# Hybrid recurrence and convolution layer: weight splits and part of the row preparation moved from VectorE and ScalarE to GpSimd in the first sweep

## The chip, the cores and the metric

The kernel runs on one core of one Trainium2 chip. The metric is the device time of one execution in microseconds. The core has TensorE (PE in the rows; its weight loads are PEld), VectorE (DVE), ScalarE (ACT), GpSimd (POOL) and SyncE (SP), which here only issues DMAs. Each engine works through a queue of its own in order; semaphores order the engines among each other.

## The reference, cut to what matters

One layer on 4096 tokens of width 1024, with 256 context tokens ahead of them:

```
h = rmsnorm(x, norm_g) * (1 + scale(c)) + shift(c)
q, zf, zb, v, ga, u, ug, gb = split(h @ w_in)            # 8 groups of 512 columns
o = hgrn2_bidir(q, v, zf, zb)                            # 4 heads x 128, both directions
y = conv_tail(depthwise_conv(u * sigmoid(ug), width 31)) # rows and columns of the 64-wide grid
m = concat(head_rmsnorm(o) * silu(ga), y * silu(gb)) @ w_out
out = rmsnorm(x + gate(c) * m, final_norm_g)
```

The recurrence is S_t = diag(f_t) S_(t-1) + k_t v_t^T, o_t = S_t^T q_t, forward and backward over the tokens, all in float32.

## The kernel before

The tokens pass in two sweeps. The **first sweep** goes forward over NB = 16 blocks of TB = 256 tokens. For each block it makes the projections q, v, the two forget gates, u and ug, runs the forward recurrence of the block, and the row part of the convolution. The **second sweep** goes back over 32 groups of 128 tokens: the backward recurrence, the gates ga and gb, the column part of the convolution, the output projection and the last norm. Projections have float32 accuracy by splitting both operands into a high and a low float16 part and running three passes of matmuls (`proj_cm` L284, `proj_v` L295).

The work of one block b in the first sweep is a set of generators, stepped in turn by `merge` in the proportion of given weights: `hgrn(b)`, `row_conv(b)`, the projections of block b+1, `prep_rows` for block b+2 (it starts after half its share of steps), and a side job from the table `side`, which prepares weights for the second sweep. What `merge` writes is the program order; the framework's scheduler then orders each engine's queue by its own timing model.

`prep_rows` (L248 to L271) loads two tiles of 128 rows. Each tile goes: SP loads `xt` (L253), ACT squares it (L256, which writes a scrap into `hl`), DVE and POOL form the reciprocal root (L257, L78; L81, L84, L85 on POOL, 128x1 each), then for two halves of 512 columns DVE multiplies (L263) and adds (L265), ACT casts to float16 (L266), DVE subtracts for the low part (L268), and SP transposes both parts into `aT` by DMA (L271).

The side jobs are: block 1 `gate_rows`, block 2 `scale_w2` twice, blocks 3 to 6 of the table `split_w2` for two weight groups, blocks 7 to 10 `split_wo` twice. Between `merge` and the scheduler the queues run about one block ahead of the table; by the trace the `split_w2` writes lie in stretches b2 to b5 and the `split_wo` writes in b6 to b9. `split_w2` loads 256 rows of a weight group into `wst`, scales and splits them (ACT L183, DVE L184) and writes both parts to DRAM as `w2d`. `split_wo` loads a gate row and a piece of `w_out` into `gw`, multiplies them (DVE L907 or L909), casts (ACT L910), subtracts (DVE L911) and writes `wod`. The tiles `hl` of all three jobs share one buffer (tag A, a single buffer), and `xt`, `wst` and `gw` share two. So the next user of `hl` waits until the DMA that read the one before is done.

The recurrence `hgrn(b)` has levels: ACT copies keys into `km` (L751), PE makes scores (L726), DVE scales and doubles (L758, L759), then two steps across larger halves (PE L779, ACT L789 and L798, DVE L768 and L769). At its end `split_keys` splits the keys into float16 parts (ACT L555, DVE L556, tile K) and SP transposes them by DMA back into X (L557); PE needs the transposed keys for `pu` (L573). SP also issues the tile writes `qbd` (X, L806), in queue order with the weight writes and loads. A stretch "b4" below is the time from one block's first write of `opd` (L825) to the next.

```
proj.append(project_v(aTs[b], d))
if b + 1 < NB:
    proj.append(project_fq(aTs[b + 1], blk[b + 1]))
if b + 2 < NB:
    proj.append(project_gu(b + 1, aTs[b + 1], blk[b + 1]))
gens.append((2 * N_UV if late_gu else N_V + N_FQ + N_GU, chain(*proj)))
if b in side:
    gens.append((26, chain(*side[b])))
if b + 2 < NB:
    gens.append((2 * N_ROWS, chain(idle(N_ROWS), prep_rows((b + 2) * TB, aTs[b + 2]))))
merge(*gens)
```

Of the kernel before, what the change touches and what calls it, by code (L numbers as in the profile page):

```python
# [9 lines left out]
F32 = mybir.dt.float32  # L10
# [4 lines left out]
ALU = mybir.AluOpType  # L15
# [24 lines left out]
R_NG, R_BM, R_LB, R_HG, R_CB, R_LG, R_LBI = 0, 8, 32, 48, 52, 56, 60  # L40
# [33 lines left out]
def rsqrt(nc, pool, out, v, n, tag, eng=None):  # L74

    eng = eng or nc.gpsimd
    y, t, h = out, pool.tile([P, n], F32, tag=tag + "t", name=tag + "t"), v
    nc.vector.tensor_scalar(y.bitcast(I32), v.bitcast(I32), -0.5, float(0x5F3759DF), ALU.mult, ALU.add)  # L78
    if n == 1:
        h = pool.tile([P, n], F32, tag=tag + "h", name=tag + "h")  # L80
        eng.tensor_scalar(h, v, -0.5, 0.0, ALU.mult, ALU.add)  # L81
    for _ in range(3):
        if n == 1:
            eng.tensor_scalar(t, y, y, h, ALU.mult, ALU.mult)  # L84
            eng.tensor_scalar(y, t, 1.5, y, ALU.add, ALU.mult)  # L85
        else:
            eng.tensor_tensor(t, y, y, ALU.mult)
            eng.tensor_tensor(t, t, v, ALU.mult)  # L88
            eng.tensor_scalar(t, t, -0.5, 1.5, ALU.mult, ALU.add)
            eng.tensor_tensor(y, y, t, ALU.mult)  # L90
# [8 lines left out]
def hymba_block(  # L99
# [3 lines left out]
    nc = tc.nc  # L103
# [12 lines left out]
    def const(shape, dt=F32, name=None):  # L116
        return cp.tile(shape, dt, tag=name, name=name)
# [6 lines left out]
    vec = const([P, NROW], name="vec")  # L124
# [34 lines left out]
    rwall = const([P, 8, 2], name="rwall")  # L159
# [17 lines left out]
    def split_chunk(hi, lo, st, g, dve=False):  # L177

        rw = rwall[:, g, 0:1]
        if dve:  # L180
            nc.vector.tensor_scalar(hi, st, rw, None, ALU.mult)
        else:
            nc.scalar.activation(hi, st, AF.Copy, scale=rw)  # L183
        nc.vector.scalar_tensor_tensor(lo, st, rw, hi, ALU.mult, ALU.subtract)  # L184

    def win_rows(g, k, n):
        return w_in[k * P : (k + n) * P, 512 * g : 512 * g + 512].rearrange("(k p) n -> p k n", p=P)
# [4 lines left out]
    with ExitStack() as s1:  # L192
# [55 lines left out]
        def prep_rows(r0, aT):  # L248

            for i in range(2):  # L250
                t = e1.tile([P, D], F32, tag="xt", name="xt", bufs=2)
                hl = e1.tile([P, 2, D], F16, tag="A", name="hl")
                nc.sync.dma_start(t, x[r0 + i * P : r0 + (i + 1) * P, :])  # L253
                yield
                ssq = sm.tile([P, 1], F32, tag="xssq", name="xssq")
                nc.scalar.activation(hl[:, 0, :].bitcast(BF16), t, AF.Square, accum_out=ssq)  # L256
                nc.vector.tensor_scalar(ssq, ssq, 1.0 / D, EPS, ALU.mult, ALU.add)  # L257
                r = sm.tile([P, 1], F32, tag="xr", name="xr")
                rsqrt(nc, sm, r, ssq, 1, "xq")
                yield  # L260
                for sl in (slice(0, 512), slice(512, D)):
                    ts = t[:, sl]
                    nc.vector.scalar_tensor_tensor(ts, ts, r, gs[:, 0, sl], ALU.mult, ALU.mult)  # L263
                    yield
                    nc.vector.tensor_tensor(ts, ts, gs[:, 1, sl], ALU.add)  # L265
                    nc.scalar.copy(hl[:, 0, sl], ts)  # L266
                    yield
                    nc.vector.tensor_tensor(hl[:, 1, sl], ts, hl[:, 0, sl], ALU.subtract)  # L268
                    yield
                for j in range(2):  # L270
                    nc.sync.dma_start_transpose(aT[:, j, :, i * P : (i + 1) * P], hl[:, j, :])  # L271
# [206 lines left out]
        gs = m1.tile([P, 2, D], F32, name="gs")  # L478
# [407 lines left out]
        def split_w2(g, i):  # L886

            t = e1.tile([P, 2 * 512], F32, tag="xt", name="wst", bufs=2)
            hl = e1.tile([P, 2, 2 * 512], F16, tag="A", name="hl")
            nc.sync.dma_start(t.rearrange("p (k n) -> p k n", n=512), win_rows(g, 2 * i, 2))  # L890
            yield
            split_chunk(hl[:, 0, :], hl[:, 1, :], t, g)
            nc.sync.dma_start(w2d[g][i], hl)
            yield

        def split_wo(k):

            for n in range(2):
                sl = slice(512 * n, 512 * n + 512)
                gw = e1.tile([P, 2, 512], F32, tag="xt", name="gw", bufs=2)  # L900
                hl = e1.tile([P, 2, 512], F32R, tag="A", name="hl")
                nc.sync.dma_start(gw[:, 0, :], gtd[:, sl])
                nc.sync.dma_start(gw[:, 1, :], w_out[k * P : (k + 1) * P, sl])
                yield
                w = gw[:, 1, :]
                if k < 4:
                    nc.vector.scalar_tensor_tensor(w, w, vec[:, R_HG + k : R_HG + k + 1], gw[:, 0, :], ALU.mult, ALU.mult)  # L907
                else:
                    nc.vector.tensor_tensor(w, w, gw[:, 0, :], ALU.mult)  # L909
                nc.scalar.copy(hl[:, 0, :], w)  # L910
                nc.vector.tensor_tensor(hl[:, 1, :], w, hl[:, 0, :].bitcast(F32), ALU.subtract)  # L911
                for i in range(2):
                    nc.sync.dma_start(wod[i][n][:, k, :], hl[:, i, :].bitcast(F32))
                yield

        side = {1: [gate_rows()], 2: [scale_w2(G_GA), scale_w2(G_GB)]}
        for i in range(4):
            side[3 + i] = [split_w2(G_GA, i), split_w2(G_GB, i)]
            side[7 + i] = [split_wo(2 * i), split_wo(2 * i + 1)]
# [35 lines left out]
        aTs[1] = new_aT(1)  # L955
        fq0 = chain(project_fq(aTs[0], blk[0]), project_gu(0, aTs[0], blk[0]))
        merge((N_CST, context_states(*cur["c"])), (N_FQ + N_GU, fq0), (5 * (N_LW - 8) // 3, lw), (N_ROWS, prep_rows(TB, aTs[1])))
        for b in range(NB):
            d = blk[b]
            if b < NB - 2:  # L960
                nc.sync.dma_start(aTd[b], aTs[b])
            late_gu = b == NB - 1
            if late_gu:
                late["gu"] = wp.tile([P, 2, T], F32, tag="pair", name="gu_all")
            gens = [(N_HGRN, hgrn(b, d)), (N_CONV * 5 // 4, chain(idle(N_CONV // 4 if late_gu else 0), row_conv(b, d)))]
            proj = [project_gu(b, aTs[b], d)] if late_gu else []
# [9 lines that stand above are left out]
                aTs[b + 2] = new_aT(b)  # L976
                gens.append((2 * N_ROWS, chain(idle(N_ROWS), prep_rows((b + 2) * TB, aTs[b + 2]))))
            if b == NB - 1:
                gens.append((N_W2, load_w2()))
            merge(*gens)  # L980
# [248 lines left out]
```

## Time and profile before

| what | value |
|---|---|
| median of 3 runs | 2219.68 us (2218.23 to 2222.2) |
| profiled execution | 2215.77 us |
| its span on the core | 2214.0 us |
| PE busy | 2083.6 us (94%) |
| DVE busy | 1749.6 us (79%) |
| ACT busy | 996.3 us (45%) |
| POOL busy | 458.5 us (21%), 1146 instructions |

The span is the time between the first and the last record of the core; the profiled execution's own time is 1.8 us above it and 3.9 us below the median of the runs. Busy time of an engine is the sum of its instructions without waits; the share is of the span. The page's slices of the span give the granted clock of TensorE in tenths, and it reads 9 nearly throughout.

### The profile page before, as it was taken

Reading aid. Unit: us, or ns where it says so; the run is one execution under the profiler, and the core shown is the slowest. Engines: PE = TensorE matmul, PEld = TensorE weight load, DVE = VectorE, ACT = ScalarE, POOL = GpSimd, SP = SyncE. Lnnn points to the kernel's source line nnn. Section 1 sums busy time; section 2 is a strip of 40 time slices with the busy share of each in tenths; the row PEclk is TensorE's granted clock in tenths of the full one; section 3 lists DMA queues with packets and bytes.
Section 4 is the critical chain, followed back from the end, with each engine's and each line's share of the span. In section 5 each row is a group of like instructions: output and inputs, shape, how many; then the busy total and the mean of one; then the engine's idle time right before and its main releaser. Section 6 shows DMA issues by size and latency. Waiting matters only on the chain. (4 is left out here: it accounts for less than half of the span.)

```text
span 2214.0 us, 54678 instructions
## 1 busy us (share of the span) xinstructions
PE 2083.6 (94%) x22334; PEld 1642.5 (74%) x22334; DVE 1749.6 (79%) x4270; ACT 996.3 (45%) x2310; POOL 458.5 (21%) x1146
## 2 busy tenths in 40 slices
PE   6999999999998999999999999978999999999997
PEld 3777778778777778778788876766677766667776
DVE  5988887897797887887898778888787887777754
ACT  4944545545535445445544543433333333333343
POOL 1110101110110110101110100044433344433332
PEclk8999999999999999999999999989999999999999
DMA  9436165324325335343322317332323322332322
GB/s 363 133 84 163 55 169 149 104 79 134 102 68 177 109 99 172 98 115 97 85 61 68 64 59 234 107 130 94 110 91 108 102 96 91 100 98 99 114 96 72
DMA packets 221476, 251.65 MB, mean 114 GB/s; under 512 B 143812, under 2 KB 147736, under 8 KB 216744
## 3 DMA queue, kind: packets, MB, share of 16 engines
q1 hardware_dynamic: 220104, 239.67, 36.4%
q0 software_dynamic: 1120, 8.49, 1.0%
q8 instruction: 175, 2.87, 0.5%
q14 instruction: 77, 0.63, 0.1%
HBM read 137.99 MB, written 76.55 MB: 97 GB/s over the span
## 5 line engine op out<-in xcount | busy, mean ns | idle before, releaser
L284 PEld LDWEIGHTS <-w 128*128 128x128 f16 x4704 | 455.8, 98 | 60.5 <-issue 2.6
L706 DVE SCALAR_TENSOR_TENSOR yr<-gu,convw,yr 128x224 f32<-128x224 f32 (+2 forms) x900 | 356.6, 444 | 0.0
L1048 DVE SCALAR_TENSOR_TENSOR ycs<-gu_all,convw,ycs 128x256 f32<-128x256 f32 (+2 forms) x828 | 343.9, 469 | 0.0
L284 PEld LDWEIGHTS <-pair 128*128 128x128 f16 x3168 | 308.5, 99 | 39.4 <-issue 0.6
L1146 PE MATMUL py<-wo,yh 128*128 128x512 f32 x1024 | 282.1, 413 | 3.8 <-ACT yh L1130 3.8
L81 POOL TENSOR_SCALAR xqh<-xssq 128x1 f32<-128x1 f32 x30 | 12.5, 418 | 1017.7 <-DVE xssq L257 1017.7
L1146 PEld LDWEIGHTS py<-wo,yh 128*128 128x128 f32 x1024 | 189.0, 192 | 43.8 <-ACT yh L1130 4.4
L284 PE MATMUL ps_z<-aT,pair 128*128 128x256 f16 x1632 | 191.1, 277 | 0.0
L1015 PE MATMUL ps_gb<-aT,w 128*128 128x256 f16 x1536 | 190.1, 273 | 0.0
L284 PE MATMUL ps_z<-aT,w 128*128 128x256 f16 x1632 | 188.3, 274 | 1.9 <-DVE aT L242 1.4
L295 PE MATMUL pv<-w,aT 128*128 128x512 f16 x816 | 184.4, 379 | 1.4 <-DVE gu L670 1.4
L751 ACT COPY km<-X 128x512 f32<-128x512 f32 x160 | 107.9, 675 | 168.2 <-DVE X L759 167.9
L284 PE MATMUL ps_u<-aT,w 128*128 128x256 f16 x1536 | 180.6, 274 | 0.0
L1003 PE MATMUL ps_ga<-w,aT 128*128 128x512 f16 x768 | 178.6, 385 | 0.0
L284 PE MATMUL ps_g<-aT,w 128*128 128x256 f16 x1536 | 178.3, 273 | 0.0
L284 PE MATMUL ps_q<-aT,pair 128*128 128x256 f16 x1536 | 172.9, 273 | 0.0
L1015 PEld LDWEIGHTS <-w 128*128 128x128 f16 x1536 | 145.5, 98 | 31.5 <-issue 15.8
L295 PEld LDWEIGHTS <-aT 128*128 128x128 f16 x816 | 77.4, 98 | 88.3 <-issue 1.6
L1146 PE MATMUL py<-wo,yl 128*128 128x512 f32 x512 | 139.6, 402 | 0.0
L1003 PEld LDWEIGHTS <-aT 128*128 128x128 f16 x768 | 72.8, 99 | 88.1 <-issue 10.4
L314 ACT ACTIVATE f<-f,lbv,oml 128x128 f32<-128x128 f32 x272 | 113.0, 485 | 0.1
L1146 PEld LDWEIGHTS py<-wo,yl 128*128 128x128 f32 x512 | 95.0, 192 | 19.1
(268 smaller groups left out, 3360.7 us busy)
## 6 DMA issues: line engine op xcount, KB each, us to landing
xt<-in_x_dram SPq DMA_DIRECT2D x64, 512.0 KB, 3.5
out_dram<-xt SPq DMA_DIRECT2D x31, 512.0 KB, 2.7
aTd<-aT SPq DMA_DIRECT2D x14, 1024.0 KB, 4.7
aT<-aTd SPq DMA_DIRECT2D x14, 1024.0 KB, 5.8
wst<-in_w_in_dram SPq DMA_DIRECT2D x16, 512.0 KB, 4.5
wod<-hl SPq DMA_DIRECT2D x32, 256.0 KB, 3.0
qbd<-X SPq DMA_DIRECT2D x31, 256.0 KB, 2.1
ubd<-ub SPq DMA_DIRECT2D x31, 256.0 KB, 2.0
```

Of the source, the lines that this page charges most:

```text
L81: eng.tensor_scalar(h, v, -0.5, 0.0, ALU.mult, ALU.add)
L284: nc.tensor.matmul(ps[:, j, :], w[:, wi, k, (ct + j) * P : (ct + j + 1) * P], aT[:, ai, k, :], start=n == 0, stop=n == 23)
L295: nc.tensor.matmul(pv, aT[:, ai, k, i * P : (i + 1) * P], W[G_V][:, wi, k, :], start=n == 0, stop=n == 23)
L314: nc.scalar.activation(fa, fa, AF.Identity, scale=oml[:, d, ct + j : ct + j + 1], bias=lbv[:, d, ct + j : ct + j + 1])
L706: nc.vector.scalar_tensor_tensor(ar[i][:, :, lo:hi], gr[i][:, :, lo + dl : hi + dl], convw[:, i, j : j + 1], ar[i][:, :, lo:hi], ALU.mult, ...
L751: nc.scalar.copy(fap(km, 0, kd), fap(Xs[gi], 0, ks))
L1003: nc.tensor.matmul(ps, aT[:, ai, k, i * P : (i + 1) * P], Wa[:, wi, k, :], start=n == 0, stop=n == 23)
L1015: nc.tensor.matmul(ps[:, j, :], Wb[:, wi, k, (ct + j) * P : (ct + j + 1) * P], aT[:, ai, k, :], start=n == 0, stop=n == 23)
L1048: nc.vector.scalar_tensor_tensor(ya, gu_all[:, i, (lo + dl) * GW : (hi + dl) * GW], convw[:, 2 + i, j : j + 1], ya, ALU.mult, ALU.add)
L1146: nc.tensor.matmul(py, y[:, k // 4, k % 4, :], W2[wi, nh][:, k, :], start=n == 0, stop=n == 23)
```

## The change

In `prep_rows` the add L265 and the subtraction L268 go to GpSimd. In `split_w2` the helper `split_chunk` (ACT cast with scale, DVE fused scale and subtract) gives way to three GpSimd instructions: a scale in place, a cast, a subtraction. In `split_wo` the products and the subtraction go to GpSimd; where DVE fused two products into one instruction (k < 4), GpSimd runs two. The cast there stays on ACT. Lines behind the second hunk move by 3, those behind the third by 2.

```diff
--- before.py
+++ after.py
@@ -262,10 +262,10 @@
                     ts = t[:, sl]
                     nc.vector.scalar_tensor_tensor(ts, ts, r, gs[:, 0, sl], ALU.mult, ALU.mult)
                     yield
-                    nc.vector.tensor_tensor(ts, ts, gs[:, 1, sl], ALU.add)
+                    nc.gpsimd.tensor_tensor(ts, ts, gs[:, 1, sl], ALU.add)
                     nc.scalar.copy(hl[:, 0, sl], ts)
                     yield
-                    nc.vector.tensor_tensor(hl[:, 1, sl], ts, hl[:, 0, sl], ALU.subtract)
+                    nc.gpsimd.tensor_tensor(hl[:, 1, sl], ts, hl[:, 0, sl], ALU.subtract)
                     yield
                 for j in range(2):
                     nc.sync.dma_start_transpose(aT[:, j, :, i * P : (i + 1) * P], hl[:, j, :])
@@ -889,7 +889,10 @@
             hl = e1.tile([P, 2, 2 * 512], F16, tag="A", name="hl")
             nc.sync.dma_start(t.rearrange("p (k n) -> p k n", n=512), win_rows(g, 2 * i, 2))
             yield
-            split_chunk(hl[:, 0, :], hl[:, 1, :], t, g)
+            rw = rwall[:, g, 0:1]
+            nc.gpsimd.tensor_scalar(t, t, rw, None, ALU.mult)
+            nc.gpsimd.tensor_copy(hl[:, 0, :], t)
+            nc.gpsimd.tensor_tensor(hl[:, 1, :], t, hl[:, 0, :], ALU.subtract)
             nc.sync.dma_start(w2d[g][i], hl)
             yield
 
@@ -904,11 +907,10 @@
                 yield
                 w = gw[:, 1, :]
                 if k < 4:
-                    nc.vector.scalar_tensor_tensor(w, w, vec[:, R_HG + k : R_HG + k + 1], gw[:, 0, :], ALU.mult, ALU.mult)
-                else:
-                    nc.vector.tensor_tensor(w, w, gw[:, 0, :], ALU.mult)
+                    nc.gpsimd.tensor_scalar(w, w, vec[:, R_HG + k : R_HG + k + 1], None, ALU.mult)
+                nc.gpsimd.tensor_tensor(w, w, gw[:, 0, :], ALU.mult)
                 nc.scalar.copy(hl[:, 0, :], w)
-                nc.vector.tensor_tensor(hl[:, 1, :], w, hl[:, 0, :].bitcast(F32), ALU.subtract)
+                nc.gpsimd.tensor_tensor(hl[:, 1, :], w, hl[:, 0, :].bitcast(F32), ALU.subtract)
                 for i in range(2):
                     nc.sync.dma_start(wod[i][n][:, k, :], hl[:, i, :].bitcast(F32))
                 yield
```

VectorE, block 4, the end of the recurrence, before; X and FL are keys, queries and decay factors, K the split keys, xt the row tile, xr its reciprocal root:

```order
L257 TENSOR_SCALAR xssq<-xssq 128x1
L78 TENSOR_SCALAR xr<-xssq 128x1
L768 TENSOR_TENSOR X<-X,FL 128x8x64
L769 TENSOR_TENSOR X<-X,FL 128x8x64
L263 SCALAR_TENSOR_TENSOR xt<-xt,xr,gs 128x512 x2
L768 TENSOR_TENSOR X<-X,FL 128x8x64
L769 TENSOR_TENSOR X<-X,FL 128x8x64
L265 TENSOR_TENSOR xt<-xt,gs 128x512
L556 SCALAR_TENSOR_TENSOR K<-X,K 128x512
L265 TENSOR_TENSOR xt<-xt,gs 128x512
L556 SCALAR_TENSOR_TENSOR K<-X,K 128x512
```

The same place now:

```order
L768 TENSOR_TENSOR X<-X,FL 128x16x32
L769 TENSOR_TENSOR X<-X,FL 128x16x32
L768 TENSOR_TENSOR X<-X,FL 128x8x64
L769 TENSOR_TENSOR X<-X,FL 128x8x64
L768 TENSOR_TENSOR X<-X,FL 128x8x64
L769 TENSOR_TENSOR X<-X,FL 128x8x64
L556 SCALAR_TENSOR_TENSOR K<-X,K 128x512 x2
L257 TENSOR_SCALAR xssq<-xssq 128x1
L78 TENSOR_SCALAR xr<-xssq 128x1
```

The first two splits of the keys stand directly behind the last doubling, and the row tile's steps follow them; two of the three kinds of row step are no longer in this queue.

GpSimd, block 4, now; before, this queue held only the three kinds of reciprocal root instruction here (L81, L84, L85):

```order
L265 TENSOR_TENSOR xt<-xt,gs 128x512 x2
L268 TENSOR_TENSOR hl<-xt,hl 128x512 x2
L894 CAST hl<-wst 128x1024
L893 TENSOR_SCALAR wst<-wst,rwall 128x1024
L895 TENSOR_TENSOR hl<-wst,hl 128x1024
L894 CAST hl<-wst 128x1024
L895 TENSOR_TENSOR hl<-wst,hl 128x1024
```

The row tile's four wide instructions and the two weight chunks stand in one row, with the next tile's L81 behind them.

ScalarE, block 8, the end of the recurrence, before; hl<-gw is the cast of `split_wo`, SC the score tile, K the split keys:

```order
L910 CAST hl<-gw 128x512
L652 ACTIVATE q<-ps_q,es 128x256 x2
L798 COPY SC<-pl 64x4x64 x3
L555 ACTIVATE K<-X 128x512
L798 COPY SC<-pl 64x4x64
L910 CAST hl<-gw 128x512
L555 ACTIVATE K<-X 128x512 x2
L666 ACTIVATE gu<-ps_g,es 128x512
```

The same place now, where the cast has line 912:

```order
L912 CAST hl<-gw 128x512
L652 ACTIVATE q<-ps_q,es 128x256 x2
L912 CAST hl<-gw 128x512
L798 COPY SC<-pl 64x4x64 x3
L555 ACTIVATE K<-X 128x512
L798 COPY SC<-pl 64x4x64
L555 ACTIVATE K<-X 128x512
```

The last cast of the block has moved from behind the first split of the keys (L555) to ahead of it, and ahead of three copies of scores.

ScalarE, block 6, the last two levels, before; L266 is the row tile's cast, km the copy of keys, L308 and L314 make the forget gate:

```order
L751 COPY km<-X 128x512
L308 ACTIVATE f<-ps_z,es 128x256 x2
L751 COPY km<-X 128x512
L314 ACTIVATE f<-f,lbv,oml 128x128 x4
L266 CAST hl<-xt 128x512 x2
L751 COPY km<-X 128x512
L308 ACTIVATE f<-ps_z,es 128x256 x2
L751 COPY km<-X 128x512
```

The same place now:

```order
L308 ACTIVATE f<-ps_z,es 128x256 x2
L751 COPY km<-X 128x512
L314 ACTIVATE f<-f,lbv,oml 128x128 x4
L266 CAST hl<-xt 128x512 x2
L751 COPY km<-X 128x512 x2
L308 ACTIVATE f<-ps_z,es 128x256 x2
```

Both copies of keys of the last level now follow the casts directly; before, one of the gate's steps stood between them.

On TensorE the number of projection matmuls (`ps_u`, `ps_g`) between the last scores of a block and its first `pu` is, before and now: block 0, 32 and 43; block 1, 48 and 53; block 2, 19 and 22; block 3, 17 and 32; block 4, 33 and 32; block 5, 33 and 32; block 6, 19 and 15; block 7, 34 and 15; block 8, 18 and 32; block 9, 25 and 32; blocks 10 to 13, 15 and 15.

On SyncE, block 4, both chunk writes (`w2d`) stood ahead of both `qbd` writes; now the second stands between them. Both stand ahead of the key transposes L557, as before.

## Rows read from the trace of the kernel before

**Rows 1.** Windows view: us, busy (instructions) per engine, PEclk, DMA share, GB/s

```profile
374.06:1036.60 662.54, 625.24 (x8707) 513.84 (x8705) 540.44 (x1237) 323.62 (x688) 69.96 (x116) 0.98 0.41 113
1036.60:1264.92 228.32, 228.15 (x3268) 188.96 (x3266) 188.28 (x440) 112.74 (x245) 21.24 (x35) 1.00 0.29 68
531.69:538.69 7.00, 7.00 (x44) 6.47 (x45) 3.81 (x8) 1.90 (x3) 0.00 (x0) 0.57 1.06 175
```

**Rows 2.** Waits of PE, first sweep: total us, times, longest us

```profile
PE pu L573 <- DMA X<-K: 27.1, 11, 4.6
PE pl L726 <- ACT km L751: 19.2, 23, 1.6
...
PE pl L779 <- DVE X L769: 2.7, 6, 1.0
```

**Rows 3.** Timeline of PE, blocks 4 and 8: start, us, line, [idle before]

```profile
524.84 3.77 PE L284 MATMUL ps_u<-aT,w 128*128 128x256 f16 x33
531.69 1.44 PE L573 MATMUL pu<-v,X 128*128 128x128 f16 x12 [3.08 <-DMA X<-K]
...
866.68 0.83 PE L573 MATMUL pu<-v,X 128*128 128x128 f16 x12 [1.38 <-DMA X<-K]
```

**Rows 4.** Timeline of DVE, block 4

```profile
515.23 1.28 DVE L184 SCALAR_TENSOR_TENSOR hl<-wst,rwall,hl 128x1024 f16<-128x1024 f32 x1 [5.48 <-ACT hl L183]
...
524.44 1.42 DVE L263 SCALAR_TENSOR_TENSOR xt<-xt,xr,gs 128x512 f32<-128x512 f32 x2 [2.24 <-POOL xr L85]
...
527.58 0.68 DVE L556 SCALAR_TENSOR_TENSOR K<-X,K 128x512 f16<-128x512 f32 x1
```

**Rows 5.** Timeline of SP (DMA issues), block 4

```profile
509.78 0.32 SPq L893 DMA_DIRECT2D w2d<-hl  x1
...
516.54 0.32 SPq L893 DMA_DIRECT2D w2d<-hl  x1
...
528.34 2.60 SPq L557 DMA_TRANSPOSE X<-K  x2
```

**Rows 6.** DVE groups by line: busy us, mean ns | idle before

```profile
L268 DVE TENSOR_TENSOR hl<-xt,hl 128x512 f16<-128x512 f32 x60 | 40.1, 683 | 0.6
...
L265 DVE TENSOR_TENSOR xt<-xt,gs 128x512 f32<-128x512 f32 x60 | 39.0, 683 | 0.0
...
L911 DVE TENSOR_TENSOR hl<-gw,hl 128x512 fp32r<-128x512 f32 x16 | 11.1, 691 | 21.3 <-ACT hl L910 21.2
...
L907 DVE SCALAR_TENSOR_TENSOR gw<-gw,vec 128x512 f32<-128x512 f32 x8 | 6.0, 750 | 5.3 <-DMA gw<-in_w_out_dram 5.3
...
L909 DVE TENSOR_TENSOR gw<-gw 128x512 f32<-128x512 f32 x8 | 5.5, 691 | 7.6 <-DMA gw<-in_w_out_dram 7.5
```

**Rows 7.** POOL groups by line, whole span

```profile
L84 POOL TENSOR_SCALAR xqt<-xr,xqh 128x1 f32<-128x1 f32 x90 | 77.4, 860 | 17.9 <-DVE xr L78 10.2 <-POOL xqh L81 0.8
...
L368 POOL MEMSET sc<- 128x256 f32 x1 | 0.3, 317 | 0.0
masks.py:199 POOL TENSOR_SCALAR_AFFINE_SELECT ident<-ident 128x128 f32<-128x128 f32 x1 | 0.3, 311 | 0.1
masks.py:197 POOL MEMSET ident<- 128x128 f32 x1 | 0.2, 205 | 0.3 <-POOLq L1215 0.3
```

**Rows 8.** Timeline of POOL, block 12

```profile
1075.00 3.06 POOL L84 TENSOR_SCALAR xqt<-xr,xqh 128x1 f32<-128x1 f32 x1
```

**Rows 9.** Timeline of ACT, blocks 4 and 8

```profile
507.29 1.15 ACT L183 ACTIVATE hl<-wst,rwall 128x1024 f16<-128x1024 f32 x1 [1.91 <-DMA aT<-hl]
...
514.05 1.15 ACT L183 ACTIVATE hl<-wst,rwall 128x1024 f16<-128x1024 f32 x1 [2.11 <-DMA w2d<-hl]
...
858.07 1.14 ACT L798 COPY SC<-pl 64x256 f32<-64x256 f32 x3
859.30 0.63 ACT L555 ACTIVATE K<-X 128x512 f16<-128x512 f32 x1
...
861.06 0.62 ACT L910 CAST hl<-gw 128x512 fp32r<-128x512 f32 x1 [0.73 <-DMA wod<-hl]
```

## Prediction

> **What bounds the kernel now.** I read the busy shares first (PE 94%), then the windows by block, then PE's waits, then the timelines of the engines that PE waits for. The eleven blocks from 374 us on fall in two kinds [rows 1]. Three plain blocks, without a side job, take 228.32 us, 76.1 each, and PE is busy in 228.15 of them: nothing but PE's own work counts there. The eight blocks with side jobs take 662.54 us, 82.8 each, which is 53.7 us above eight plain ones; PE stands idle in 37.3 us of that. So all that the change can win is in these eight blocks (and in the two before), and it lies in what PE waits for. In the other blocks, where PE is full, lighter loads on VectorE and ScalarE win nothing, and only a new wait can count.
>
> PE waits longest for the transposed keys, 27.1 us in 11 waits; then for the copies of keys in the levels, 19.2 us in 23 waits; and for L769 on VectorE, 2.7 us [rows 2]. Block 4 shows how a key wait comes about. PE ends the matmuls at 528.61 and starts `pu` at 531.69, 3.08 us late [rows 3], since SP issued the transposes at 528.34 [rows 5], right behind the split of the keys at 527.58 on VectorE [rows 4]. Ahead of that split VectorE had waited 5.48 us for ScalarE's scaled cast of a weight chunk and 2.24 us for a reciprocal root from POOL [rows 4]. Neither wait has to do with the keys; they are ahead of it in the queue. After the pause PE runs 7 us at a granted clock of 0.57 [rows 1], close to the lower of its levels, 1.2 of 2.4 GHz: another 7 x 0.43 = 3.0 us.
>
> **What the moved work costs.** VectorE loses 40.1 + 39.0 + 11.1 + 6.0 + 5.5 us [rows 6] and eight chunk splits of 1.28 us [rows 4], 112 us in all; ScalarE loses eight casts of 1.15 us [rows 9], 9.2 us. None of it is on the path by itself. POOL had no wide two-input instruction, so its price is bounded. Two fills of 128 and 256 elements took 205 and 317 ns [rows 7]: 0.875 ns per element written and 93 ns fixed; 512 elements would be 0.54 us, 1024 would be 0.99, which is the lower bound. The select over 128 elements, one read and one write, took 311 ns [rows 7]: 1.70 ns per element, so a read is worth 0.83, and two reads and a write 2.53. The upper bounds are 1.39 us (two inputs, 512), 2.68 (two inputs, 1024), 1.84 (one input, 1024) and 0.96 (one input, 512). The select is the nearer row, as it reads and writes; I take a little under it, 1.2, 2.2, 1.5 and 0.85 us. POOL then gets 120 x 1.2 (rows) + 8 x 5.2 (`split_w2`) + 8 x 0.85 + 32 x 1.2 (`split_wo`) = 231 us, bounds 110 and 270. POOL is 70 us busy in the 662.54 of the side blocks [rows 1], so it has the room; what counts is latency and queue order.
>
> **Blocks 4 and 5 (gain).** The walk starts where the buffer came free, 507.29 us [rows 9]. POOL casts to 508.8, scales the next chunk to 510.3, subtracts to 512.5. From the issue of a chunk's write to the next cast passed 514.05 - 509.78 = 4.3 us [rows 5, 9]; so the second cast runs from 516.8 to 518.3, the subtraction to 520.5, and its write is issued at 520.6, 4.1 us later than now (516.54 [rows 5]). It stands ahead of the key transposes in SP's queue. PE arrives at 528.61 and needs them 3.35 us earlier (528.34 to 531.69 [rows 3, 5]), by 525.3. That leaves 4.7 us; with the upper bounds (two one-input instructions and a subtraction, the trip, one and one) the write goes at 522.5, still in time. The row tile before it, whose four moved steps cost 4 x (1.2 - 0.683) = 2.1 us more, may take half of the slack. On VectorE the wait of 5.48 us is gone with its instruction, and the row tile's train now stands behind the first two splits. Gain per block: the pause and the slow clock, 3.08 + 3.0. Block 5 reads like block 4. **Term: -12.2 us**, with the ends 0 and -12.2.
>
> **Blocks 0, 1, 3 and 6 (gain).** The new order puts more projection matmuls ahead of the first `pu` in blocks 0, 1 and 3 (43 for 32, 53 for 48, 32 for 17), and in block 6 the keys are split ahead of a cast that is now later. Of the 27.1 us of waits, 4.6 are block 6's [rows 2] and about 2.3 each is the mean of the other blocks. 33 such matmuls take 3.77 us [rows 3], so eleven more cover 1.25. But a matmul moved ahead is missing as cover further on. I take -2 for blocks 0 and 1 and -3 for 3 and 6. **Term: -5**, ends 0 and -11.
>
> **Blocks 8 and 9 (loss).** In block 8 the last cast of `split_wo` started at 861.06, when the write before it was done, behind the first key split at 859.30 on ScalarE [rows 9]. Now it stands ahead of three score copies (1.14 us) and of that split. Its POOL pieces are slower: (1.2 + 1.2) for (0.691 + 0.691) on a chunk, and 1.1 us more on the chunk ahead, so it starts at about 863.2 and the first key split at about 863.2 + 0.6 + 1.1 = 864.9, 5.6 us later than now. PE already waited 1.38 us there [rows 3], some of the delay is covered by matmuls that can go ahead, and block 9 has the same order. **Term: +9** for both; ends 0 (the queue settles as before) and +12.
>
> **The levels (loss).** In each of 13 blocks the two row casts (L266) stand ahead of both copies of keys of one level on ScalarE, and they now wait for two additions on POOL, 2.4 us for 1.37, and for POOL's earlier row steps. PE's waits for those copies are 0.8 us on average, 1.6 at most [rows 2]. I take +0.4 per block; the worst is one full further wait of 1.7. **Term: +5**, ends 0 and +22. The 2.7 us of waits for L769 [rows 2] go with VectorE's lighter queue: **-2.7**, ends 0 and -2.7.
>
> **Sum.** -12.2 - 5 + 9 + 5 - 2.7 = -5.9 us. The working comes from the execution of 2215.77 us (span 2214.0), which is 3.9 below the median; the same difference on the median of 2219.7 gives **2214 us**. About 0.2% (4.4 us) is what a measurement of this kernel can tell from no change.
>
> **A rule that speaks against it.** POOL's tiny instructions (128x1) have a mean of 860 ns [rows 7], and one took 3.06 us [rows 8], over three times that; in such stretches VectorE runs two-input instructions back to back. So the two engines do get in each other's way, and what is seen is POOL losing. The Trainium skill, page "SBUF — State Buffer", section "Who interferes with whom", has VectorE instructions with two SBUF inputs contend with GpSimd instructions that read SBUF, by an exclusive lock under which the loser stands for the whole instruction. By that rule VectorE would be held by each wide POOL instruction in its turn; the trace agrees on POOL's side (3.06 us) and no run here shows VectorE's. The Trainium skill, page "GPSIMD Engine Reference", section "3.1 Elementwise — side-by-side cycle accounting", gives 4497 ns on GpSimd for a float32 addition of 2048 elements; an estimate from that page is 1.1 us for 512, and the sum would be the same.
>
> **Rivals.** (1) *VectorE is held.* If each wide POOL instruction stops VectorE for its own time, a row tile costs VectorE 4 x 1.2 in place of 4 x 0.683 us, 2.1 more, in the levels where PE follows VectorE closely (VectorE is 82% busy in the side blocks [rows 1]). One tile of each block falls there: 13 x 2.1 = +27. With half of the gain in blocks 4 and 5 (-6), +9 for blocks 8 and 9, -5 for the rest: +25, **2245 us**, 2224 to 2265. It decides as soon as more than about half of POOL's time is added to VectorE's chain. For it: POOL's long instructions [rows 8]. Against: so far VectorE wins. (2) *All gain, no price.* All 27.1 us of key waits and the 2.7 of L769 go [rows 2], the levels have cover: 2219.7 - 29.8 = **2190 us**. Against it: blocks 8 and 9, whose order is worse. (3) *It moves nothing*, 2219.7: the key waits of blocks 4 and 5 go and their 18 us come back in later key waits and the levels, as their ends (+12 and +22) allow, or the keys there are late for another reason.
>
> **Chances.** Forecast, 2200 to 2215: 0.40. All gain: 0.08. Nothing moved (2215 to 2224): 0.20. VectorE held: 0.32. Faster by over 0.2%: 0.48, within: 0.20, slower: 0.32. The range 2190 to 2245 leaves out half of the last case and half of the second, 0.2 together; the likeliest case alone has 2200 to 2215.
>
> **What would show it.** Right: wide POOL two-input instructions of 128x512 near 1.2 us; the key waits of blocks 4 and 5 gone, and the granted clock after them near 1; waits of over 3 us for keys in blocks 8 and 9; plain blocks within 0.5 us of 76.1. Wrong: mean times of VectorE's two-input instructions (0.683 us) well up, or plain blocks of 78 us and more (rival 1); a second chunk's write after 525 us (the first term falls); POOL instructions of over 2 us at 128x512, by which the row tiles and the casts on ScalarE come late.

## The result, and the profile after

The changed kernel takes 2282.28 us (median of 4 runs, 2277.61 to 2284.66) against 2218.95 us of the kernel before on the same chip: ratio 1.0282, 95% interval 1.026 to 1.0304, 63 us slower. The forecast was 2214 us and a range of 2190 to 2245. The profiled span grew from 2214.0 to 2279.2 us, by 65.2.

The line of busy times after; its columns are busy time, share of the span and instructions of each engine:

```profile
PE 2105.6 (92%) x22334; PEld 1651.4 (72%) x22334; DVE 1782.7 (78%) x4110; ACT 989.5 (43%) x2302; POOL 748.3 (33%) x1330
```

VectorE should have dropped from 1749.6 by the 112 us that were moved, to 1637.6. It stands at 1782.7: it gave its work away and is 33 us busier, so its other instructions grew by 145 us. GpSimd rose by 290 us; 231 were forecast and 270 was the upper bound.

The windows after, cut at the same places of the program as the first two of [rows 1], and the 7 us from block 4's first `pu` on:

```profile
393.11:1091.55 698.44, 633.87 (x8673) 515.71 (x8672) 557.96 (x1129) 318.60 (x684) 271.19 (x245) 0.97 0.40 110
1091.55:1327.09 235.54, 228.68 (x3267) 189.16 (x3265) 196.60 (x420) 112.49 (x245) 54.25 (x55) 1.00 0.28 66
562.53:569.53 7.00, 6.90 (x74) 6.37 (x74) 6.32 (x10) 3.78 (x7) 4.90 (x3) 1.00 0.45 88
```

The eight side blocks lose 698.4 - 662.5 = 35.9 us, the three plain ones 235.5 - 228.3 = 7.2 us. The stretch ahead of them (its end moves from 374.06 to 393.11) loses 19.0 and the rest of the program 3.0; together that is the 65. Plain blocks, where PE was idle for 0.2 us in all, now show 6.9 us of idle time. Over the whole program 43.2 of the 65.2 us are idle time of PE, and 22.0 are longer busy time for the same 22334 instructions (2105.6 against 2083.6): the mean granted clock is 0.968 in place of 0.978, and 2083.6 x 0.978 / 0.968 is 2105.

PE's waits in the first sweep, to be read beside [rows 2]:

```profile
PE pl L726 <- ACT km L751: 45.5, 29, 3.7
PE pu L573 <- DMA X<-K: 20.2, 10, 3.9
PE pu L573 <- DVE v L564: 16.0, 7, 4.3
PE pl L726 <- DVE kap L738: 7.5, 2, 5.4
PE pl L779 <- DVE X L769: 5.1, 3, 4.2
```

The key waits fell by 7 us, from 27.1 to 20.2. The waits for copies of keys rose by 26, and three others that were absent or small rose by 25.6 together. The new ones name VectorE, or ScalarE behind it.

### The profile page after: what moved, and what is told of

It reads as the page before. It is cut to its first block, busy times and chain, and to the rows that moved or that the text cites. A ratio compares the mean times of both kernels' runs of the same rounds, so it can differ in the third digit from the quotient of the medians.

```text
span 2279.2 us, 54772 instructions
## 1 busy us (share of the span) xinstructions
PE 2105.6 (92%) x22334; PEld 1651.4 (72%) x22334; DVE 1782.7 (78%) x4110; ACT 989.5 (43%) x2302; POOL 748.3 (33%) x1330
## 5 line engine op out<-in xcount | busy, mean ns | idle before, releaser
L706 DVE SCALAR_TENSOR_TENSOR yr<-gu,convw,yr 128x224 f32<-128x224 f32 (+2 forms) x900 | 369.7, 459 | 0.0
L284 PEld LDWEIGHTS <-pair 128*128 128x128 f16 x3168 | 313.8, 100 | 47.9 <-issue 4.1
L81 POOL TENSOR_SCALAR xqh<-xssq 128x1 f32<-128x1 f32 x30 | 11.6, 386 | 636.3 <-DVE xssq L257 636.3
L284 PE MATMUL ps_z<-aT,pair 128*128 128x256 f16 x1632 | 201.3, 285 | 0.0
L295 PE MATMUL pv<-w,aT 128*128 128x512 f16 x816 | 188.3, 385 | 0.3 <-DVE gu L670 0.2
L768 DVE TENSOR_TENSOR X<-X,FL 128x512 f32<-128x512 f32 x64 | 64.0, 1001 | 93.8 <-PE pl L780 93.7
L81 POOL TENSOR_SCALAR hrh<-hv 128x1 f32<-128x1 f32 x31 | 8.6, 277 | 357.4 <-DVE hv L1158 282.5
```

Source lines behind the costliest of these rows:

```text
L284: nc.tensor.matmul(ps[:, j, :], w[:, wi, k, (ct + j) * P : (ct + j + 1) * P], aT[:, ai, k, :], start=n == 0, stop=n == 23)
L295: nc.tensor.matmul(pv, aT[:, ai, k, i * P : (i + 1) * P], W[G_V][:, wi, k, :], start=n == 0, stop=n == 23)
L706: nc.vector.scalar_tensor_tensor(ar[i][:, :, lo:hi], gr[i][:, :, lo + dl : hi + dl], convw[:, i, j : j + 1], ar[i][:, :, lo:hi], ALU.mult, ...
L768: nc.vector.tensor_tensor(xa, xa, half(f, FL, h, 1), ALU.mult)
```

## Where the time went

Block 12, a plain one, shows the mechanism instruction by instruction. VectorE there in the kernel before, behind the row tile's multiplication L263 (timeline: start, duration, line, shape):

```profile
1080.60 1.29 DVE L265 TENSOR_TENSOR xt<-xt,gs 128x512 f32<-128x512 f32 x2
1081.81 0.68 DVE L758 TENSOR_TENSOR X<-X,FL 128x512 f32<-128x512 f32 x1
1082.41 0.68 DVE L759 TENSOR_TENSOR X<-X,FL 128x512 f32<-128x512 f32 x1
1083.01 0.68 DVE L268 TENSOR_TENSOR hl<-xt,hl 128x512 f16<-128x512 f32 x1
1083.61 0.68 DVE L758 TENSOR_TENSOR X<-X,FL 128x512 f32<-128x512 f32 x1
1084.21 0.68 DVE L759 TENSOR_TENSOR X<-X,FL 128x512 f32<-128x512 f32 x1
1084.82 0.44 DVE L762 COPY_PREDICATED SD<-masks,pl 128x256 f32<-128x256 uint8 x1
```

The same stretch after, where the row steps are GpSimd's:

```profile
1214.30 1.75 DVE L758 TENSOR_TENSOR X<-X,FL 128x512 f32<-128x512 f32 x1
1215.98 1.75 DVE L759 TENSOR_TENSOR X<-X,FL 128x512 f32<-128x512 f32 x1
1217.66 1.65 DVE L758 TENSOR_TENSOR X<-X,FL 128x512 f32<-128x512 f32 x1
1219.23 1.64 DVE L759 TENSOR_TENSOR X<-X,FL 128x512 f32<-128x512 f32 x1
1220.79 0.43 DVE L762 COPY_PREDICATED SD<-masks,pl 128x256 f32<-128x256 uint8 x1
```

GpSimd in the same microseconds:

```profile
1213.86 3.33 POOL L265 TENSOR_TENSOR xt<-xt,gs 128x512 f32<-128x512 f32 x2 [0.93 <-ACT f L314]
1217.15 3.17 POOL L268 TENSOR_TENSOR hl<-xt,hl 128x512 f16<-128x512 f32 x2
```

Before, VectorE came from behind L263 to the masked copy L762 in 4.22 us (1080.60 to 1084.82), with four doublings and three row steps. After, it takes 6.49 us (1214.30 to 1220.79) for the four doublings alone. Each doubling takes 1.64 to 1.75 in place of 0.68 us, while four GpSimd instructions of 1.6 us are under way beside them (1213.86 to 1220.32). The masked copy L762 behind them is 0.43 us as ever. For its second copy of keys ScalarE waits 2.57 us for the last L759, and PE waits 1.97 us for ScalarE:

```profile
1220.96 0.62 ACT L751 COPY km<-X 128x512 f32<-128x512 f32 x1 [2.57 <-DVE X L759]
```

```profile
1221.63 0.46 PE L726 MATMUL pl<-X,km 128*32 128x32 f32 x32 [1.97 <-ACT km L751]
```

The releaser of ScalarE is VectorE's L759, not GpSimd's L265: here PE is late because VectorE is held, and not because ScalarE's row casts wait for GpSimd. Over the whole program the doublings read, after:

```profile
L758 DVE TENSOR_TENSOR X<-X,FL 128x512 f32<-128x512 f32 x128 | 110.7, 865 | 5.5 <-PE pl L726 3.6 <-ACT f L314 1.9
L759 DVE TENSOR_TENSOR X<-X,FL 128x512 f32<-128x512 f32 x128 | 108.3, 846 | 0.0
L768 DVE TENSOR_TENSOR X<-X,FL 128x512 f32<-128x512 f32 x64 | 64.0, 1001 | 93.8 <-PE pl L780 93.7
...
L769 DVE TENSOR_TENSOR X<-X,FL 128x512 f32<-128x512 f32 x64 | 61.1, 955 | 0.0
```

The mean of the same four groups before was 682 to 684 ns. These four alone grew by 82 us (344.1 against 262.2).

The moved instructions on GpSimd:

```profile
L265 POOL TENSOR_TENSOR xt<-xt,gs 128x512 f32<-128x512 f32 x60 | 94.4, 1591 | 37.1 <-ACT K L555 11.0 <-ACT f L314 9.2 <-issue 9.2
L268 POOL TENSOR_TENSOR hl<-xt,hl 128x512 f16<-128x512 f32 x60 | 88.9, 1499 | 0.7 <-ACT hl L266 0.5
...
L893 POOL TENSOR_SCALAR wst<-wst,rwall 128x1024 f32<-128x1024 f32 x8 | 25.3, 3159 | 28.8 <-DMA wst<-in_w_in_dram 25.3 <-DVE rwall L156 3.5
...
L910 POOL TENSOR_SCALAR gw<-gw,vec 128x512 f32<-128x512 f32 x8 | 16.1, 2016 | 15.3 <-DMA gw<-in_w_out_dram 15.3
...
L894 POOL CAST hl<-wst 128x1024 f16<-128x1024 f32 x8 | 8.3, 1037 | 23.5 <-DMA aT<-hl 12.7 <-DMA w2d<-hl 10.7
```

The 128x512 subtractions and additions take 1.4 to 1.6 us where 1.2 was taken and 1.39 was the upper bound; the shortest took 1.27 (L265) and 1.15 us (L268), so part of it may be waiting for VectorE, whose doublings stand beside them in the block 12 rows. The cast is cheap (1.04), but a product with a column of factors is not: 3.16 us for 128x1024 and 2.02 us for 128x512, far over the bounds of 1.84 and 0.96.

## The experiments

Theory A is that each wide GpSimd instruction holds VectorE. Its rivals: B, that GpSimd's slower chains make casts, writes and transposes late; C, that the new order of the queues costs by itself. "Held" in the table is VectorE's busy time in the one profiled execution above what its own instructions would take at the times of the kernel before. Behind each time stand the ratio and its 95% interval.

| run | GpSimd instructions added | time against before | VectorE held |
|---|---|---|---|
| only_rows | 120, two inputs | +58.0 us (1.0262, 1.0235 to 1.0288) | 1781.7 - 1670.5 = 111 us |
| only_add | 60, two inputs | +36.2 us (1.016, 1.0144 to 1.0175) | 1762.9 - 1710.6 = 52 us |
| only_sub | 60, two inputs | +30.5 us (1.0134, 1.0117 to 1.015) | 1741.1 - 1709.5 = 32 us |
| only_w2 | 24, wide | +3.2 us (1.0019, 1.0004 to 1.0034) | 1756.3 - 1739.3 = 17 us |
| only_wo | 40, wide | +1.1 us (1.0006, 0.9991 to 1.0022) | 1743.1 - 1727.0 = 16 us |
| extra_two | 120, two constant inputs | +103.3 us (1.0463, 1.0445 to 1.0481) | 1860.8 - 1749.6 = 111 us |
| extra_tied | 120, two inputs | +107.8 us (1.0481, 1.0465 to 1.0496) | 1863.3 - 1749.6 = 114 us |
| extra_tied_copy | 120, one input | +39.2 us (1.0169, 1.015 to 1.0189) | 1787.8 - 1749.6 = 38 us |
| extra_one | 120, one constant input | +26.9 us (1.0118, 1.01 to 1.0137) | 1787.2 - 1749.6 = 38 us |
| extra_fill | 120, no input | +7.0 us (1.0032, 1.002 to 1.0044) | 1756.4 - 1749.6 = 7 us |

### One part of the change alone

only_rows keeps the first hunk of the change alone.

> The row steps L265 and L268 on GpSimd, both weight splits as before. Theory A (each wide two-input GpSimd instruction holds VectorE's two-input instructions, which then take 1.6 to 1.75 us in place of 0.68 while one runs, and PE follows VectorE in the levels): most of the loss is here, about +46 us (the stretches without side work lost 2.3, 2.9 and 2.0 us in the changed kernel, 2.4 x 8 in the side blocks, and 19 up to the third block). Theory B (GpSimd's slower chains make casts, writes and transposes late): the weight chunks are what is late, so at most +25 us here. Theory C (the new order of the queues costs by itself): no more than +10 us.

It measured +58.0 us, more than theory A's +46 and more than twice B's limit. Nearly the whole loss is the row steps.

only_w2 has the second hunk alone, only_wo the third.

> Only split_w2 on GpSimd. Theory A: 8 subtractions of 128x1024 are the only wide two-input instructions, VectorE loses 10 us of its own work in exchange; +6 us (0 to +12). Theory B: the second chunk's write comes late and the key transposes behind it: +15 us or more, with key waits of over 3 us in stretches b2 to b5.

> Only split_wo on GpSimd. Theory A: 32 wide two-input instructions of 128x512 and 8 products with a column, +10 us (5 to 15), in the stretches b6 to b8. Theory B: the cast on ScalarE waits for GpSimd ahead of the key splits: +20 us, all of it as key waits.

They cost +3.2 and +1.1 us. The first lies in A's range (0 to +12); for the second A said +5 at the least, so it missed: VectorE was held by 16 us there as well, but PE did not follow it in those places, or the order gave it back. Which of the two is open. B fell in both. The three parts sum to 58.0 + 3.2 + 1.1 = 62.3 us, and the whole change has 63.3: they hardly touch each other.

### Half of the row steps

```
only_add:
-                    nc.vector.tensor_tensor(ts, ts, gs[:, 1, sl], ALU.add)
+                    nc.gpsimd.tensor_tensor(ts, ts, gs[:, 1, sl], ALU.add)
only_sub:
-                    nc.vector.tensor_tensor(hl[:, 1, sl], ts, hl[:, 0, sl], ALU.subtract)
+                    nc.gpsimd.tensor_tensor(hl[:, 1, sl], ts, hl[:, 0, sl], ALU.subtract)
```

> Only the addition L265 on GpSimd (60 instructions); the subtraction L268 stays on VectorE. ScalarE's casts, which stand ahead of the copies of keys in its queue, wait for these additions. Theory A (VectorE held): half of the 120 instructions, so about half of the 58 us of the run with both, +22 to +36. Theory B (late casts): nearly the whole, +45 or more, since the casts wait for the additions alone.

> Only the subtraction L268 on GpSimd (60 instructions); the addition stays on VectorE, so the casts on ScalarE do not wait for wide GpSimd work. Theory A: +22 to +36, the other half. Theory B: under +10, since nothing but the row transposes, a block ahead of their use, waits for the subtractions.

+36.2 and +30.5 us. Nothing urgent waits for the subtractions, yet they cost nearly as much as the additions: that is A, and B's "under +10" falls. PE's waits for transposed keys did not grow there either (26.4 us, 27.1 before). VectorE's total does not decide it: in only_sub VectorE is busy 8.5 us less than before (1741.1 against 1749.6), and the time is still 30.5 us longer. What counts is which of its instructions are held.

The addition came out at the very edge of A's range, 5.7 us above the subtraction. Its waits speak for holding and not for late casts: PE's waits for copies of keys, which stand behind the casts, hardly changed from the 19.2 us of [rows 2], and those for transposed keys, 27.1 there, grew:

```profile
PE pu L573 <- DMA X<-K: 43.1, 12, 5.3
PE pl L726 <- ACT km L751: 20.0, 22, 1.9
```

In block 4 of this run the two doublings ahead of the first split of the keys took 0.69 us each before, and take 1.76 and 1.75 now; GpSimd's two additions (546.92 to 550.25) are under way beside them:

```profile
547.37 1.76 DVE L768 TENSOR_TENSOR X<-X,FL 128x512 f32<-128x512 f32 x1
549.05 1.75 DVE L769 TENSOR_TENSOR X<-X,FL 128x512 f32<-128x512 f32 x1
```

So one cause makes different things late, depending on what stands beside GpSimd's instructions. The two halves sum to 66.7, a little over the 58.0 of both.

### Wide GpSimd work that nobody needs

The additional instruction stands behind each row step on VectorE; `pad` is a scratch tile.

```
+                pad = e1.tile([P, 512], F16, tag="pad", name="pad")
extra_two:        nc.gpsimd.tensor_tensor(pad, gs[:, 0, sl], gs[:, 1, sl], ALU.add)
extra_tied:       nc.gpsimd.tensor_tensor(pad, ts, gs[:, 1, sl], ALU.add)
extra_tied_copy:  nc.gpsimd.tensor_copy(pad, ts)
extra_one:        nc.gpsimd.tensor_scalar(pad, gs[:, 0, sl], 2.0, None, ALU.mult)
extra_fill:       nc.gpsimd.memset(pad, 1.0)
```

> The kernel before, and beside each L265 and L268 on VectorE an additional GpSimd addition of two constant 128x512 inputs into a scratch tile (120 in all) that nothing reads. Nothing is moved, so VectorE keeps its work. Theory A: VectorE's two-input instructions are held as in the changed kernel, and time rises by 40 to 60 us. Theory B: nobody waits for these instructions but the next row tile's reciprocal root, so within 8 us of the kernel before. Theory C: within 8 us, whichever sign.

The size was even larger, +103.3 us, but not spread as expected. As nothing but constants feeds these additions, the scheduler put them at the front: nearly all ran in the first 310 us, and there nearly the whole loss lies (the first `opd` write of block 0 comes at 309.7 against 210.2 us, and block 0's stretch is 6.3 us longer). From block 1 on the stretches are as before, the plain ones at 76.3, 75.7 and 76.1 us. In the plain ones VectorE and ScalarE also have the same order as before, so this run says nothing on theory C. One half of the additions on GpSimd:

```profile
L265 POOL TENSOR_TENSOR pad<-gs 128x512 f16<-128x512 f32 x60 | 94.3, 1572 | 9.0 <-DMA gs<-gsd 5.5
```

VectorE's row convolution, the same 60 instructions, in the stretch from 100 us to block 0's first `opd`, in the kernel before and then in this run:

```profile
L706 DVE SCALAR_TENSOR_TENSOR yr<-gu,convw,yr 128x196 f32<-128x196 f32 (+14 forms) x60 | 24.1, 443 | 0.0
```

```profile
L706 DVE SCALAR_TENSOR_TENSOR yr<-gu,convw,yr 128x196 f32<-128x196 f32 (+14 forms) x60 | 54.4, 945 | 0.0
```

443 ns become 945, with no change in the work. The timeline of VectorE in this run shows that a tiny instruction is held too, and the row of GpSimd behind it what stood in the way:

```profile
212.16 1.22 DVE L534 TENSOR_TENSOR FL<-FL 128x8 f32<-128x8 f32 x1
```

```profile
212.05 1.31 POOL L265 TENSOR_TENSOR pad<-gs 128x512 f16<-128x512 f32 x1
```

This multiplication over 128x8 elements (L534) took 1.22 us; in the kernel before four of these average 0.158. It stood for nearly a whole GpSimd instruction.

> The kernel before, and behind each L265 and L268 on VectorE an additional GpSimd addition that reads the row tile's half and a constant and writes a scratch tile (120 in all), so that it runs where the row steps run, in every block. Nothing reads the scratch; only the row tile's buffer is given back later. Theory A: VectorE keeps its own work and is held as well, +40 to +80 us, spread over the blocks, stretches without side work +2 us or more each. Theory B: within 8 us of the kernel before.

Reading the row tile pins the additions to the places of the row steps. +107.8 us, above A's range; plain blocks take 84.9, 83.3 and 81.3 us in place of 76. In these three blocks VectorE and ScalarE run the same instructions in the same order as in the kernel before. Still VectorE is busy 209.6 us there, against 188.3 in [rows 1], and the blocks take 21.2 us longer:

```profile
1120.56:1370.04 249.48, 233.83 (x3267) 191.37 (x3265) 209.59 (x440) 112.77 (x245) 53.29 (x55) 0.98 0.28 63
```

The order cannot make the same instructions busy for longer, and nobody reads what the additions write, so B and C fall as the cause in the plain blocks. In the side blocks the change also reorders VectorE's queue; what that adds there is not shown apart. Each addition holds VectorE for 114 / 120 = 0.95 us.

> The same 120 places, but each additional GpSimd instruction copies the row tile's half (one input) to the scratch tile. If any wide GpSimd instruction that reads SBUF holds VectorE: +20 to +50 us, by its length against the two-input one's. If only a two-input GpSimd instruction holds it: within 6 us, and VectorE's two-input instructions stay at 0.68 us.

> As the run with the two-input additions on constants, but each of the 120 GpSimd instructions multiplies one constant half by a number (one input). From the copies (1 us each, +39 us for 120): +35 to +60 us, by its length; under +10 if a one-input instruction with arithmetic does not hold VectorE.

> As the run with the two-input additions on constants, which all ran in the first 310 us, but each of the 120 GpSimd instructions fills the scratch tile (no input). If a GpSimd instruction holds VectorE because it reads SBUF: within 6 us of the kernel before, and VectorE's mean times unchanged. If any wide access holds it: +20 to +50 us.

A copy holds too: +39.2 us, 0.32 us each. So the second input is not what makes GpSimd hold VectorE, but it makes it much worse. A product with a number, one input, is as long as an addition (1.7 us) and yet costs only +26.9, below the expected range, 0.31 us of holding each. Additions and products on constants ran in the same part of the program (from 64 to about 330 us), so the hold follows the inputs read, not the duration. A fill, without inputs, cost +7.0, one us over what was expected of "no hold", 0.06 us each. The fills waited for nothing and ran from 6 to 91 us, ahead of block 0, so their time is not to be set against the others place by place. One half of the copies and of the products on GpSimd:

```profile
L265 POOL CAST pad<-xt 128x512 f16<-128x512 f32 x60 | 65.2, 1087 | 83.7 <-DVE xt L265 81.8
```

```profile
L265 POOL TENSOR_SCALAR pad<-gs 128x512 f16<-128x512 f32 x60 | 101.4, 1690 | 8.3 <-DMA gs<-gsd 5.2
```

Beside the fills VectorE's instructions with two SBUF inputs kept their times, but products with a column of factors (one input) did not. Between 6 and 91 us, in the kernel before and then with the fills:

```profile
L184 DVE SCALAR_TENSOR_TENSOR w<-w,rwall,w 128x1024 f16<-128x1024 f32 x8 | 9.8, 1280 | 1.0 <-ACT w L183 1.0
...
L181 DVE TENSOR_SCALAR w<-w,rwall 128x1024 f16<-128x1024 f32 x4 | 2.8, 749 | 0.0
```

```profile
L184 DVE SCALAR_TENSOR_TENSOR w<-w,rwall,w 128x1024 f16<-128x1024 f32 x8 | 9.7, 1271 | 0.0
...
L181 DVE TENSOR_SCALAR w<-w,rwall 128x1024 f16<-128x1024 f32 x4 | 3.7, 962 | 0.1
```

The products and casts of this kind (L181, L220, L242 and L600) grew by 4.0 us, most of the 6.8 that VectorE was held.

### The other direction

```
-                rsqrt(nc, sm, r, ssq, 1, "xq")
+                rsqrt(nc, sm, r, ssq, 1, "xq", nc.vector)
```

> A try in the other direction: the kernel before, with the row tiles' reciprocal root (seven 128x1 instructions per tile, 210 in all) on VectorE in place of GpSimd. VectorE's 39.5 us of waits for it go and 210 x 0.15 = 31 us of work come. Theory A (sharing costs): 0 to -12 us, if the key splits behind those waits come earlier. Against it: VectorE takes on work in the levels, +5.

It measured 2214.79 us, 2.6 below the kernel before on the same chip (0.9985, 0.9973 to 0.9998). That is inside the 0.2% that tells a change from none, but it is the only version below the kernel before. The waits for copies of keys halve against [rows 2]; the key waits grow, so the splits of the keys did not gain what was expected:

```profile
PE pu L573 <- DMA X<-K: 35.6, 14, 4.1
...
PE pl L726 <- ACT km L751: 9.1, 17, 1.3
```

## Why the prediction was wrong, step by step

**The step that failed** is "None of it is on the path by itself", with what was said of POOL, "so it has the room; what counts is latency and queue order". GpSimd had the room. But its wide instructions take VectorE's time while they run, about 0.93 us of each two-input 128x512 instruction (111 us over 120), against 0.683 us that moving it frees. With both kinds of row step moved, VectorE loses a quarter of a microsecond per step instead of winning 0.68. The subtractions alone hold it for 0.53 us each, less than they free, and still cost 30.5 us: the loss falls where PE follows VectorE, as the row steps run beside the doublings of the levels. The forecast's sum has no term for this; it counts VectorE's queue as lighter only (the -2.7 for L769). Nor has it one for the granted clock behind new pauses, which is 22.0 of the 65.2 us.

**The rule was on the table.** The rows showed GpSimd's tiny instructions standing for up to 3.06 us while VectorE ran [rows 8]. From this I took that "so far VectorE wins", and put it against the rival. Tiny instructions could not show the reverse: once a wide one is under way, VectorE stands. The block 12 rows show 1.64 to 1.75 us for 0.68 us of work. The Trainium skill, page "SBUF — State Buffer", section "Who interferes with whom", says just this of both sides: an exclusive lock, and the loser waits for the whole instruction. On GpSimd's side the traces agree, and on VectorE's too, with 1.22 us for 128x8 elements.

**The rival that came true, and its size.** Rival 1 had the mechanism and a chance of 0.32, and gave 2245 (2224 to 2265). It counted one tile per block at 4 x (1.2 - 0.683) = 2.1 us. In the plain blocks the estimate held: 7.2 / 3 = 2.4 us per block, of which the key copies' wait is 1.97 us in block 12. It was too small for the rest, and the measured time lies beyond the rival's range as well: the side blocks lost 35.9 / 8 = 4.5 each, and the stretch ahead of block 2 lost 19.0, where 2.1 a block had been counted. PE is late in several places of the first sweep; the seven waits for the split of the values are all new. How much of the rest is the new order of the queues stays open.

**Blocks 4 and 5** (-12.2). At the keys block 4 went as the walk said: PE starts `pu` at 562.53 with no wait, and the 7 us behind it have a granted clock of 1.00, the level of 2.4 GHz, where [rows 1] had 0.57. The second chunk's write was issued 9.8 us after the first (6.8 before [rows 5]), and the transposes are ahead of their need:

```profile
544.74 0.32 SPq L896 DMA_DIRECT2D w2d<-hl  x1
...
554.54 0.83 SPq L896 DMA_DIRECT2D w2d<-hl  x1
...
556.78 11.35 SPq L557 DMA_TRANSPOSE X<-K  x4
```

In block 5 a key wait of 2.06 us is left. "Block 5 reads like block 4" was also wrong on the clock: in the kernel before, the 7 us behind block 5's wait had a granted clock of 1.00, so the 3.0 us counted for it were not there to win:

```profile
614.71:621.71 7.00, 7.00 (x74) 6.47 (x75) 4.89 (x11) 2.75 (x5) 0.00 (x0) 1.00 0.90 202
```

And the stretch that ends with block 4's first `opd` did not get shorter: it takes 84.9 us, 2.2 more than before. PE waits there 4.8 us for copies of keys (0.7 before) and 1.4 us for the split of the values.

**Blocks 8 and 9** (+9). The direction was right, the size of the term too large. The last cast did go ahead of the key split, at 906.12 and 907.68 us, and block 8's key wait rose from 1.38 [rows 3] to 3.95; block 9's is 3.87, and was 2.98:

```profile
914.93 1.44 PE L573 MATMUL pu<-v,X 128*128 128x128 f16 x12 [3.95 <-DMA X<-K]
```

So the pauses are 2.6 + 0.9 = 3.5 us. The clock comes on top: in the 7 us from block 8's first `pu` it is 0.63, and was 1.00 before, another 2.6 us; behind block 9's it is 0.76 and was 0.78:

```profile
914.93:921.93 7.00, 7.00 (x47) 6.65 (x48) 6.32 (x10) 3.02 (x5) 5.16 (x4) 0.63 0.69 91
```

The term is then some 6 us. The stretches that end with the first `opd` of blocks 8 and 9 grew by 13.1 and 5.1 us; 6.6 and 2.2 of that are there in only_rows too, where `split_wo` is as before. All key waits together fell by 6.9 us; the terms on them, as pauses alone (-6.2, -5 and +9), summed to -2.2.

**The levels** (+5, ends 0 and +22). The waits for copies of keys rose by 26.3 us, beyond the end, for another reason than given: not the casts behind GpSimd's additions, but VectorE's own doublings. In 42.6 of the 45.5 us the copy that PE waits for had itself waited for VectorE's L759; only 2.9 us stand behind a copy that followed directly on a cast. With them came 16.0 us for the split of the values (L564), 7.2 more for `kap` and 2.4 more for L769, which was forecast to vanish.

**The unknown prices.** Of the four taken, 1.2 (two inputs, 512) measured 1.39 to 1.59 and 2.2 (two inputs, 1024) measured 2.17. 1.5 was one price for a cast and a product of 128x1024, which are 1.04 and 3.16; 0.85 measured 2.02. The estimate of 1.1 us for an addition was too short as well: none took under 1.27. No row of GpSimd before had a wide product with a column.

## What to carry to other kernels

Moving a wide elementwise step from VectorE to GpSimd frees VectorE only if the two do not run at the same time: here 0.68 us were freed and 0.93 us held for each 128x512 step with both kinds moved, and where less was held than freed (0.53 us, subtractions alone) the kernel lost time all the same. Count a GpSimd instruction that reads SBUF as work of VectorE too, and put it where nobody waits for VectorE, or leave it. A small GpSimd instruction that is starved is the sign of this sharing; it says nothing on who will lose when that instruction is wide.

## What the runs showed of the hardware

- VectorE instructions with a single SBUF input stand as well: beside the additions on constants, two copies of 128x4 elements (L807) averaged 0.69 us against 0.16, and one product with a column (L858, 128x1024) took 1.76 us against 0.73.
- VectorE instructions that read PSUM did not stand: the masked copy L762 (0.434 against 0.433 us) and L670 (0.742 against 0.743) kept their times in the same stretch.
- GpSimd fills, which read nothing, left VectorE's two-input instructions alone (L184, 1.27 us against 1.28) but lengthened its products with a column (L181, 0.96 us against 0.75).
- Two instructions of one shape and nearly one length on GpSimd, the addition (1.57 us) and the product with a number (1.68 us), hold VectorE for 0.93 and 0.31 us.
